# A two-layer hybrid decoder: the later projections with tokens stationary, and first loads and bias rows on other queues

## The chip, the cores and the metric

The kernel runs as one program on one core of a Trainium2 chip. The metric is the device time of the program in microseconds (us), as the median of several executions. One execution was also taken by the hardware profiler; all rows below come from it.

## The reference: what is computed

The input is x with 256 tokens of 2048 channels. Two layers follow each other, each with an RMS norm in front and a residual addition behind.

```python
h = rmsnorm(x, norm_g[0])                      # layer 0: dilated attention
proj = h @ a_w_in                              # 2048 x 20480
q, k, v of 3 groups x 16 heads x 128, z = split(proj)
q, k = head_rms(q) * gain, head_rms(k) * gain
o_g = softmax(q k^T / sqrt(128) + t5_bias, window and dilation of g) v
o = merge of the 3 groups by their softmax denominators
x = x + (o * silu(z)) @ a_w_out                # 2048 x 2048

h = rmsnorm(x, norm_g[1])                      # layer 1: Conformer convolution
a, ga, z = split(h @ b_w_in + b_in, 3)         # 2048 x 6144
u = causal_depthwise_conv(a * sigmoid(ga), width 31) + conv_b
u = layernorm(u) * ln_g + ln_b                 # over channels
x = x + (silu(u) * silu(z)) @ b_w_out + b_out  # 2048 x 2048
```

All of it is float32. The four weight matrices hold 30,720 rows of 2048 values, some 252 MB, and each is read once.

## The kernel before

**Chunks.** All weights come as 480 chunks of 128 x 1024 values (512 KB), read in a fixed order n: 320 for `a_w_in` (n below `N_A`), 32 for `a_w_out` (from `N_A` to `N_WO`), 96 for `b_w_in` (to `N_VI`), 32 for `b_w_out`. `stage(n)` (L108) fetches chunk n over SP's queue into `raw`, ScalarE (ACT) rounds it to `hi`, and `lo` = raw - hi is made by VectorE (DVE) or GpSimd (POOL), as `low_engine` (L92) says. Each of the three tiles has five buffers. The activations are split in the same way, and each product is three matmuls: high by high, low by high, high by low.

**The order is written by hand.** The main loop (L845 to L860) goes once over all chunks. For chunk n it stages chunk n + 3, issues the matmuls of chunk n, and then runs the functions that `at(n, ...)` has put at this step. Each engine works through its own instructions in this order, so an instruction that waits holds up all behind it on its engine. SP's queue holds the weight loads and all other loads and stores, with few exceptions.

**Attention stage (n below 320).** Eight sets of two heads, each with five column groups of eight chunks. `project` (L275) keeps 128 tokens stationary (`xh`, `xl`) and moves 512 weight columns, so a chunk is 12 matmuls of 512 columns into two accumulators of 128 tokens x 512. For q and k they are normalised, turned on TensorE by four transposes (`qk_turn`, L323) and split. The scores, softmax and values of the set before run between the chunks. The first eight chunks also load, scale and split x (`x_split`, L149; `load_first`, L154). From step 10 to 30 the T5 bias table is made in four parts: `bias_load` (L222) fetches a part of the one-hot and mask rows, `bias_rows` (L241) multiplies and adds, and `bias_store` (L250) writes it to memory over SP's queue. `load_bias` (L262) reads it back per head.

**The later stages.** `project_out` (L515) and `project_b` (L621) keep 128 x 128 weights stationary and move 256 tokens, so a chunk is 24 matmuls of 256 columns (L526 to L529 for the first half of an output projection, `products`, L537, elsewhere). Results have channels on the partitions. Accumulators come from four PSUM banks in turn (`acc`); two banks (`t`) take transposes and small sums, and `s` and `o` the scores and values.

- After `a_w_out`: `residual`, `square_sum`, `h_split` (L567 to L582) make x1, its squares' sum and the two parts of the second layer's input. The factor r1 of the norm is summed over partitions and spread to all of them by TensorE (`r1_sums`, `r1_spread`, L603 to L613), and is multiplied into every result of `b_w_in` (L646, L653, L797).
- Under `b_w_in` the convolution runs on VectorE: for each of 16 channel tiles 29 taps of 128 x 256 (`conv_tap`, L687), in two half sums in PSUM that are merged (L691). A list `line` with planned costs spreads them over the chunks (`run_line`, L636). POOL adds up the sums and squares for the layer norm (`gather`, L729). The mean of the first six tiles is taken off early (`mid_sums`). After the last tile `ln_sums` and, one chunk later, `ln_spread` (L744, L758) make the statistics with TensorE, VectorE and POOL, and `norm` and what follows it (L771 to L794) prepare the input of `b_w_out`, two channel tiles at a time.
- `store` (L826) adds x1 to each result and writes it over SP's queue, channels first; the host turns the output.

Of the kernel before, what the change touches and what calls it, by code (L numbers as in the profile page):

```python
# [17 lines left out]
P = 128  # L18
# [23 lines left out]
def hybrid_kernel(ctx: ExitStack, tc: tile.TileContext, x_perm, x_tok, x_nat, vecs, rel, onehot, maskrow,  # L42
                  w_in, w_out, v_in, v_out, out):
# [10 lines left out]

    def acc_tile(name):
        return bank("acc", name, 4)

    def t_tile(name):
        return bank("t", name, 2)
# [15 lines left out]
    units, z_next = [], 0  # L75
    for j in range(KT):
        units += [2 * j, 2 * j + 1]
        if j % 2 and j > 2:
            units.append(32 + z_next)
            z_next += 1  # L80
    units += [32 + j for j in range(z_next, KT)]

    def source(n):
        if n < N_A:
            return w_in[n]
        if n < N_WO:
            return w_out[n - N_A]
        if n < N_VI:
            return v_in[2 * units[(n - N_WO) // 2] + (n - N_WO) % 2]
        return v_out[n - N_VI]  # L90

    def low_engine(n):  # L92
        if n < N_WO + 8:
            return nc.gpsimd if N_A + 3 <= n < N_A + 16 else nc.vector
# [13 lines left out]
    def stage(n):  # L108
# [40 lines left out]
    def x_split(k, xr):  # L149
        g0 = vec[:, V_G0 + k:V_G0 + k + 1]  # L150
        nc.scalar.activation(xh[:, k, :], xr, AF.Copy, scale=g0)
        nc.vector.scalar_tensor_tensor(xl[:, k, :], xr, g0, xh[:, k, :].bitcast(F32), op0=ALU.mult, op1=ALU.subtract)  # L152

    def load_first():  # L154

        xr = apool.tile([P, 2, S], F32, tag="sc", name="xr0", bufs=2)
        raw, hi, lo = new_chunk(0)
        for i in range(2):
# [6 lines left out]
        for i in range(2):  # L165
            sl = slice(i * 512, (i + 1) * 512)
            nc.scalar.copy(hi[:, sl], raw[:, sl])
            x_split(i, xr[:, i, :])
            nc.vector.tensor_tensor(lo[:, sl], raw[:, sl], hi[:, sl].bitcast(F32), op=ALU.subtract)
# [52 lines left out]
    def bias_load(f):  # L222
        if f == 0:
            brow["rb"] = apool.tile([N_BUCKETS, NG * NH], F32, name="rb")
            nc.sync.dma_start(brow["rb"], rel)
            brow["oh"] = apool.tile([N_BUCKETS, 1024], F32, tag="bt", name="oh", bufs=2)
            brow["row"] = apool.tile([NH, 1024], F32, tag="bt", name="row", bufs=2)
            brow["oh_r"] = apool.tile([N_BUCKETS, 1024], F32R, tag="pp", name="oh_r", bufs=1)
        nc.sync.dma_start(brow["oh"], onehot[:, f * 1024:(f + 1) * 1024])
# [715 lines left out]
```

## Time and profile before

| | |
|---|---|
| median of 3 executions | 1452.47 us (1452.23 to 1452.49) |
| the profiled execution | 1452.36 us |
| its span in the trace | 1450.6 us |
| TensorE busy | 1442.3 us (99%) |
| VectorE, ScalarE, POOL busy | 960.2, 727.0, 423.7 us |
| DMA | 271.28 MB, mean 187 GB/s |

The span is the time from the first to the last instruction of the trace. Busy time is the time in which at least one instruction of the engine was at work. Matmuls overlap one another, so the durations of single matmuls add up to more than the time that they take.

### The profile page before, as it was taken

How to read it: one execution, taken by the hardware profiler on the slowest of the kernel's cores; microseconds unless marked ns; L12 is line 12 of the kernel's file. 1: busy time of each engine (PE TensorE's matmuls, PEld its weight loads, DVE VectorE, ACT ScalarE, POOL GpSimd, SP SyncE). 2: the span in 40 equal slices, each digit the busy share in tenths (PEclk: the TensorE clock that was granted, in tenths of full speed). 3: DMA queues.
4: the chain of work that ended last, by engine and by line, in shares of the span. 5: the costliest groups of instructions: out<-in, count | busy, mean ns of one | idle time of the engine just before them, and what ended most of it. 6: DMA issues, size and time to landing. Idle time of an engine off the chain costs nothing.

```text
span 1450.6 us, 22407 instructions
## 1 busy us (share of the span) xinstructions
PE 1442.3 (99%) x8524; PEld 1275.6 (88%) x8524; DVE 960.2 (66%) x1542; ACT 727.0 (50%) x1027; POOL 423.7 (29%) x339
## 2 busy tenths in 40 slices
PE   9999999999999999999999999999999999999999
PEld 7778888888888888888888888889999999999999
DVE  6656765765676576576567657646758989997621
ACT  7445554454455455445445545444545545555632
POOL 0210020011011002001001100207217979998544
PEclk9999999999999999999999999999999999999999
DMA  9458556557556655755755665566564655555544
GB/s 360 139 202 251 161 185 206 173 164 217 170 164 197 194 165 181 207 170 170 216 169 164 197 193 165 180 189 218 163 197 165 204 162 182 192 180 184 184 158 142
DMA packets 108699, 271.28 MB, mean 187 GB/s; under 512 B 42416, under 2 KB 44720, under 8 KB 108592
## 3 DMA queue, kind: packets, MB, share of 16 engines
q1 hardware_dynamic: 108160, 269.58, 58.2%
q8 instruction: 67, 1.10, 0.3%
q14 instruction: 40, 0.33, 0.1%
q10 hardware_dynamic: 432, 0.28, 0.1%
HBM read 267.46 MB, written 2.36 MB: 186 GB/s over the span
## 4 chain that ended last, share of the span: by engine, by line
PE 98%; DMA 1%; DVE 0%; ACT 0%; issue 0%; SPq 0%; POOL 0%; POOLq 0%; ACTq 0%
PE acc L290 60%; PE b L541 6%; PE b L542 6%; PE b L543 6%; PE psq L327 1%; PE wow L526 1%; PE vo L543 1%; PE vo L542 1%; PE vo L541 1%; PE vow L529 1%; PE vow L528 1%; PE vow L526 1%; PE wo L543 1%; PE wo L541 1%; PE wo L542 1%; PE wow L528 1%
## 5 line engine op out<-in xcount | busy, mean ns | idle before, releaser
L114 ACT CAST hi<-raw 128x1024 fp32r<-128x1024 f32 x479 | 497.0, 1048 | 292.7 <-PE acc L290 164.2
L117 DVE TENSOR_TENSOR lo<-raw,hi 128x1024 fp32r<-128x1024 f32 x358 | 441.3, 1234 | 282.2 <-ACT hi L114 275.7
L290 PE MATMUL acc<-hi,xh 128*128 128x512 f32 x1280 | 506.0, 397 | 0.1
L290 PE MATMUL acc<-lo,xh 128*128 128x512 f32 x1280 | 497.4, 391 | 0.8 <-DVE lo L117 0.8
L290 PE MATMUL acc<-hi,xl 128*128 128x512 f32 x1280 | 495.9, 389 | 0.0
L117 POOL TENSOR_TENSOR lo<-raw,hi 128x1024 fp32r<-128x1024 f32 x121 | 294.0, 2453 | 120.4 <-ACT hi L114 101.6
L290 PEld LDWEIGHTS acc<-lo,xh 128*128 128x128 f32 x1280 | 240.1, 188 | 53.4 <-DVE lo L117 1.2
L290 PEld LDWEIGHTS acc<-hi,xh 128*128 128x128 f32 x1280 | 240.5, 188 | 49.0 <-issue 2.0
L290 PEld LDWEIGHTS acc<-hi,xl 128*128 128x128 f32 x1280 | 240.8, 188 | 47.1 <-DVE xl L152 0.2
L129 POOL TENSOR_SCALAR rq<-ss 128x4 f32<-128x4 f32 x48 | 10.9, 226 | 789.7 <-DVE ss L309 787.8
L541 PE MATMUL b<-hh,hi 128*128 128x256 f32 x768 | 217.8, 284 | 0.0
L542 PE MATMUL b<-hl,hi 128*128 128x256 f32 x768 | 217.3, 283 | 0.0
L543 PE MATMUL b<-hh,lo 128*128 128x256 f32 x768 | 217.3, 283 | 0.0
L688 DVE SCALAR_TENSOR_TENSOR c<-u,vec,c 128x256 f32<-128x256 f32 x464 | 187.4, 481 | 3.5 <-ACT c L684 3.5
L542 PEld LDWEIGHTS b<-hl,hi 128*128 128x128 f32 x768 | 147.4, 192 | 0.0
L541 PEld LDWEIGHTS b<-hh,hi 128*128 128x128 f32 x768 | 147.4, 192 | 0.0
L543 PEld LDWEIGHTS b<-hh,lo 128*128 128x128 f32 x768 | 147.4, 192 | 0.0
L403 ACT ACTIVATE pr<-sc,m 128x512 f32<-128x512 f32 x32 | 23.1, 723 | 100.8 <-DVE m L401 100.8
L340 DVE TENSOR_TENSOR qk<-psq,qk 128x256 fp32r<-128x256 f32 x48 | 20.3, 422 | 50.6 <-ACT qk L339 50.6
L338 ACT CAST qk<-psq 128x256 fp32r<-128x256 f32 x48 | 17.9, 372 | 64.1 <-PE psq L327 63.6
L130 POOL TENSOR_TENSOR rq<-rq,nhalf 128x4 f32<-128x4 f32 x48 | 48.4, 1008 | 4.0
L422 ACT CAST pp<-pt 128x512 fp32r<-128x512 f32 x32 | 18.8, 587 | 44.1 <-PE pt L414 42.8
(167 smaller groups left out, 1668.0 us busy)
## 6 DMA issues: line engine op xcount, KB each, us to landing
raw<-w_in SPq DMA_DIRECT2D x319, 512.0 KB, 4.2
raw<-v_in SPq DMA_DIRECT2D x96, 512.0 KB, 3.3
raw<-w_out SPq DMA_DIRECT2D x32, 512.0 KB, 4.2
raw<-v_out SPq DMA_DIRECT2D x32, 512.0 KB, 4.1
bt<-btab SPq DMA_DIRECT2D x64, 128.0 KB, 5.8
x_tok<-x_tok SPq DMA_DIRECT2D x4, 512.0 KB, 9.4
x<-x_nat SPq DMA_DIRECT2D x4, 512.0 KB, 6.3
out_t<-ob SPq DMA_DIRECT2D x16, 128.0 KB, 1.8
```

Source lines behind the costliest of these rows:

```text
L114: nc.scalar.copy(hi, raw)
L117: low_engine(n).tensor_tensor(lo, raw, hi.bitcast(F32), op=ALU.subtract)
L130: nc.gpsimd.tensor_tensor(dst, dst, nhalf[:, :n], op=ALU.pow)
L290: nc.tensor.matmul(acc[b], lhsT=(xl if p == 1 else xh)[:, k, sl], rhs=wl if p == 2 else wh, start=k == 0 and p == 0, stop=k == KT - 1 and ...
L340: nc.vector.tensor_tensor(ql, ps[:, 0:2], qh.bitcast(F32), op=ALU.subtract)
L403: nc.scalar.activation(u.pr.rearrange("p a b -> p (a b)"), sc, AF.Exp, bias=u.m[:, 1:2], accum_out=u.m[:, 2:3])
L526: nc.tensor.matmul(acc, lhsT=wh, rhs=mh[:, m, :], start=m == 0 and ct % 2 == 0, stop=False, skip_group_check=True)
L528: nc.tensor.matmul(acc, lhsT=wh, rhs=ml[:, m, :], start=False, stop=False, skip_group_check=True)
L541: nc.tensor.matmul(acc, lhsT=wh, rhs=mh[:, k, :], start=k == 0, stop=False)
L542: nc.tensor.matmul(acc, lhsT=wh, rhs=ml[:, k, :], start=False, stop=False)
L543: nc.tensor.matmul(acc, lhsT=wl, rhs=mh[:, k, :], start=False, stop=k == KT - 1)
L688: nc.vector.scalar_tensor_tensor(c[t % 2], u[:, t:t + S], vec[:, cw + t:cw + t + 1], c[t % 2], op0=ALU.mult, op1=ALU.add)
```

## The change

All four parts of the change come together.

1. The three later projections keep 128 tokens stationary and move 512 weight columns, as the attention stage does: `three` and `pair` replace `products`. Weights are laid out for it by the host (`_groups`). Results now have tokens on the partitions.
2. So x1 is turned by TensorE for the second layer's input (`x_turn`), and each group of 512 columns of `b_w_in` is emptied by ACT with the factor r1 (`take_group`) and turned (`turn_group`). r1 is summed along the free axis by ACT (`accum_out`). The output needs no turn by the host, and the bias `b_out` is added as a row (`bias_fetch`, `bias_add`).
3. During `b_w_in` one of the four accumulator banks holds the sums of the layer norm, and VectorE adds them up there instead of POOL. The two half sums of a channel tile share one bank. `CHUNK`, the planner's time of a chunk, goes from 2.64 to 2.72.
4. The first three chunks are rounded and split in halves (`split_halves`); the first part of `vec` comes over POOL's queue; the one-hot and mask rows come in two whole loads, at steps 11 and 12, and the table's parts are stored over ACT's queue.

```diff
+    turns = {"acc": 0, "t": 0}
+    ring = [0, 1, 2, 3]
     def acc_tile(name):
-        return bank("acc", name, 4)
+        turns["acc"] += 1
+        return bank(f"acc{ring[turns['acc'] % len(ring)]}", name, 1)
...
     def stage(n):
...
         nc.sync.dma_start(raw, source(n))
+        if n < LEAD:
+            split_halves(n, raw, hi, lo, xr)
+            return
...
+    def split_halves(n, raw, hi, lo, xr):
+        for i in range(2):
+            sl = slice(i * 512, (i + 1) * 512)
+            nc.scalar.copy(hi[:, sl], raw[:, sl])
+            x_split(2 * n + i, xr[:, i, :])
+            nc.vector.tensor_tensor(lo[:, sl], raw[:, sl], hi[:, sl].bitcast(F32), op=ALU.subtract)
...
     def x_split(k, xr):
-        nc.scalar.activation(xh[:, k, :], xr, AF.Copy, scale=g0)
+        if k == 0:
+            nc.vector.tensor_scalar(xh[:, k, :], xr, g0, None, op0=ALU.mult)
+        else:
+            nc.scalar.activation(xh[:, k, :], xr, AF.Copy, scale=g0)
...
     def load_first():
+        nc.gpsimd.dma_start(vec[:, :V_HEAD], vecs[:, :V_HEAD])
...
-            if i == 0:
-                nc.scalar.dma_start(vec[:, :V_HEAD], vecs[:, :V_HEAD])
...
+            brow["oh"] = bpool.tile([N_BUCKETS, 4096], F32, tag="yl", name="oh")
+            nc.sync.dma_start(brow["oh"], onehot)
+        else:
+            brow["row"] = bpool.tile([NH, 4096], F32, tag="yh", name="row")
+            nc.sync.dma_start(brow["row"], bass.AP(tensor=maskrow.tensor, offset=maskrow.offset, ap=[[0, NH], [1, 4096]]))
...
     def bias_store(f):
-        nc.sync.dma_start(btab[:, f * 1024:(f + 1) * 1024], brow["row"])
+        sl = slice(f * 1024, (f + 1) * 1024)
+        nc.scalar.dma_start(btab[:, sl], brow["row"][:, sl])
-    for f in range(4):
-        at(10 + 5 * f, bias_load, f)
...
+    for i in range(2):
+        at(11 + i, bias_load, i)
+    for f, e in enumerate((17, 21, 23, 25)):
+        at(e - 1, bias_split, f)
+        at(e, bias_rows, f, 0)
+        at(e + 1, bias_rows, f, 1)
+        at(e + 2, bias_store, f)
...
+    def three(acc, xh_, xl_, wh, wl, first, last):
+        nc.tensor.matmul(acc, lhsT=xh_, rhs=wh, start=first, stop=False)
+        nc.tensor.matmul(acc, lhsT=xl_, rhs=wh, start=False, stop=False)
+        nc.tensor.matmul(acc, lhsT=xh_, rhs=wl, start=False, stop=last)
+    def pair(accs, hi, lo, kc, mh, ml, blocks_first):
+        order = [(i, b) for i in range(2) for b in range(2)]
+        if blocks_first:
+            order.sort(key=lambda x: x[1])
+        for i, b in order:
+            k, cs, ts = 2 * kc + i, slice(i * 512, (i + 1) * 512), slice(b * P, (b + 1) * P)
+            three(accs[b], mh[:, k, ts], ml[:, k, ts], hi[:, cs], lo[:, cs], k == 0, k == KT - 1)
...
+    def x_turn(q):
+        f.pt[q] = t_tile(f"px{q}").rearrange("p (c t) -> p c t", c=2)
+        for c in range(2):
+            for b in range(2):
+                ct = 2 * q + c
+                nc.tensor.transpose(f.pt[q][:, c, b * P:(b + 1) * P], f.x1[:, b, ct * P:(ct + 1) * P], ident)
...
     def project_b(n):
...
+        g, kc = divmod(n - N_WO, 8)
+        if kc == 0:
+            if g == 0:
+                ring[:] = [i for i in ring if i != 3]
+                open_convolution()
+            acc_b[g] = [acc_tile(f"b{g}_{b}") for b in range(2)]
+        pair(acc_b[g], hi, lo, kc, f.hh, f.hl, kc in (0, 7))
...
+    def take_group(g):
+        accs = acc_b.pop(g)
+        ev_b[g] = []
+        for b in range(2):
+            ev = f.pool.tile([P, 512], F32, tag="ev", name=f"ev{g}_{b}", bufs=4)
+            nc.scalar.activation(ev, accs[b], AF.Copy, scale=f.r1[:, b:b + 1])
+            ev_b[g].append(ev)
+    def turn_group(g, part, t):
+        ps = ps_g[g, part] = t_tile(f"pg{g}_{part}", t).rearrange("p (c t) -> p c t", c=2)
+        for c in range(2):
+            for b in range(2):
+                ct = 2 * part + c
+                nc.tensor.transpose(ps[:, c, b * P:(b + 1) * P], ev_b[g][b][:, ct * P:(ct + 1) * P], ident)
...
     def conv_first(j, u, cw, c):
-        tags = (("s", "o"), ("t", "t"))[j % 2]
-        c += [bank(tags[i], f"c{j}_{i}", 2 if tags[i] == "t" else 1)[:, :S] for i in range(2)]
+        ps = bank(("s", "o")[j % 2], f"c{j}", 1)
+        c += [ps[:, :S], ps[:, S:]]
...
+    def gather(j, sq):
+        out_ = f.sb if j == KT - 1 else f.sums
+        if j > HALF_J:
+            nc.vector.tensor_tensor(out_[:, S:], f.sums[:, S:], f.d[:, j, :], op=ALU.add)
+        nc.vector.tensor_tensor(out_[:, :S], f.sums[:, :S], sq, op=ALU.add)
+        if j == KT - 1:
+            ring[:] = [0, 1, 2, 3]
+            at(f.n + 1, ln_sums)
...
+    for g in range(NB):
+        e = N_WO + 8 * g + 7
+        at(e, take_group, g)
+        if g < NGLU:
+            at(e + 1, turn_group, g, 1, 1)
+            at(e + 1, turn_group, g, 0, 0)
+            at(e + 2, glu, g)
         else:
...
+            for part in range(2):
+                at(e + 1 + 2 * part, turn_group, g, part, 1)
+                at(e + 2 + 2 * part, z_silu, g, part)
+    def store(cg):
+        accs = oacc.pop(cg)
+        for b in range(2):
+            o = f.pool.tile([P, 512], F32, tag="ev", name=f"ob{cg}_{b}", bufs=4)
+            for h in range(1 + (cg == 3 and b == 1)):
+                sl = slice(h * S, (h + 1) * S) if cg == 3 and b == 1 else slice(0, 512)
+                c0 = cg * 512
+                nc.vector.tensor_tensor(o[:, sl], accs[b][:, sl], f.x1[:, b, c0 + sl.start:c0 + sl.stop], op=ALU.add)
+                (nc.sync, nc.scalar)[h].dma_start(out[b * P:(b + 1) * P, c0 + sl.start:c0 + sl.stop], o[:, sl])
```

## Rows read from the trace of the kernel before

**Rows 1.** The page: busy time of the engines, and the chain by engine.

```profile
PE 1442.3 (99%) x8524; PEld 1275.6 (88%) x8524; DVE 960.2 (66%) x1542; ACT 727.0 (50%) x1027; POOL 423.7 (29%) x339
...
PE 98%; DMA 1%; DVE 0%; ACT 0%; issue 0%; SPq 0%; POOL 0%; POOLq 0%; ACTq 0%
```

**Rows 2.** Waits of TensorE: for whom, us in total, times, longest.

```profile
PE psq L327 <- DVE qn L319: 1.4, 1, 1.4
...
PE psq L327 <- DVE row L248: 0.8, 1, 0.8
```

**Rows 3.** Groups by form: out<-in, xcount | busy us, mean ns | idle before.

```profile
L327 PE MATMUL psq<-ident,qn 128*128 128x128 f32 x192 | 28.9, 273 | 2.2 <-DVE qn L319 1.4 <-DVE row L248 0.8
```

**Rows 4.** The chain in the attention stage: start us, us, what.

```profile
215.63 0.44 PE psq L327 x4
216.07 2.78 PE acc L290 x12
...
219.29 38.13 PE acc L290 x168
```

**Rows 5.** Timeline of TensorE, and the last addition: start us, us, what.

```profile
215.47 0.60 PE L327 MATMUL psq<-ident,qn 128*128 128x128 f32 x4
215.82 0.48 PE L290 MATMUL acc<-hi,xh 128*128 128x512 f32 x1
...
1355.19 0.28 PE L526 MATMUL vow<-bh,hi 128*128 128x256 f32 x1
...
1447.23 0.28 PE L543 MATMUL vo<-bh,lo 128*128 128x256 f32 x1
...
1447.55 0.42 DVE L828 TENSOR_TENSOR ob<-vo,x 128x256 f32<-128x256 f32 x1 [5.33 <-PE vo L543]
```

**Rows 6.** SP's wait for the table (us, times, longest), and ACT behind it.

```profile
SPq L251 <- DVE row L248: 48.6, 4, 13.5
...
89.31 1.05 ACT L114 CAST hi<-raw 128x1024 fp32r<-128x1024 f32 x1 [7.25 <-DMA raw<-w_in]
```

**Rows 7.** Timeline of the start, and small loads: KB, us to landing.

```profile
5.25 0.51 ACT L151 ACTIVATE xh<-xr,vec 128x256 fp32r<-128x256 f32 x1 [0.34 <-DMA vec<-vecs]
5.66 0.60 ACT L167 CAST hi<-raw 128x512 fp32r<-128x512 f32 x1
6.19 0.68 DVE L169 TENSOR_TENSOR lo<-raw,hi 128x512 fp32r<-128x512 f32 x1
...
7.87 1.05 ACT L114 CAST hi<-raw 128x1024 fp32r<-128x1024 f32 x1 [1.11 <-DMA raw<-w_in]
9.36 0.88 DVE L152 SCALAR_TENSOR_TENSOR xl<-xr,vec,xh 128x256 fp32r<-128x256 f32 x2 [1.48 <-ACT xh L151]
11.43 0.73 PE L290 MATMUL acc<-lo,xh 128*128 128x512 f32 x2 [0.80 <-DVE lo L117]
...
vec<-vecs ACTq DMA_DIRECT2D x1, 19.0 KB, 4.0
rb<-rel SPq DMA_DIRECT2D x1, 6.0 KB, 10.1
```

**Rows 8.** Timeline of the layer norm's statistics: VectorE and TensorE.

```profile
1334.98 2.34 DVE L755 SCALAR_TENSOR_TENSOR rn<-st_ln,rn 128x2 f32<-128x2 f32 x1 [1.12 <-POOL rn L130]
1336.09 0.60 PE L600 MATMUL ps_rn<-ident,rn 128*128 128x128 f32 x4
1337.37 0.71 PE L600 MATMUL ps_rn<-ident,rn 128*128 128x128 f32 x4 [0.68 <-DVE rn L755]
```

**Rows 9.** Taps by group and in order of time; a window's busy us by engine.

```profile
L688 DVE SCALAR_TENSOR_TENSOR c<-u,vec,c 128x256 f32<-128x256 f32 x464 | 187.4, 481 | 3.5 <-ACT c L684 3.5
...
1201.33 2.04 DVE L688 SCALAR_TENSOR_TENSOR c<-u,vec,c 128x256 f32<-128x256 f32 x5
...
1110.00:1320.00 210.00, 210.00 (x1753) 210.00 (x1753) 192.91 (x487) 111.92 (x164) 195.68 (x116) 1.00 0.56 184
```

**Rows 10.** ACT's copy of a whole bank out of PSUM, as a group.

```profile
L349 ACT ACTIVATE vh<-acc,r 128x512 fp32r<-128x512 f32 x16 | 10.8, 688 | 8.5 <-PE acc L290 8.5
```

More of the change, by code (lines that the diff above doesn't have):

```diff
@@ L71, in at @@
         steps.setdefault(n, []).append((fn, args))
[L75 to L81, printed above, removed]
+    NGLU = 8
+    NB = 12
     def source(n):
@@ L161, in load_first @@
             nc.scalar.dma_start(xr[:, i:i + 1], x_perm[:, i:i + 1, :])
-            if i == 0:
-                nc.scalar.dma_start(vec[:, :V_HEAD], vecs[:, :V_HEAD])
         warm_up()
[L165 to L169, printed above, removed]
+        split_halves(0, raw, hi, lo, xr)
     def load_x(c):
@@ L238, in bias_split @@
             nc.vector.tensor_tensor(brow["lo"], brow["rb"], brow["hi"].bitcast(F32), op=ALU.subtract)
-        nc.scalar.copy(brow["oh_r"], brow["oh"])
+        brow["oh_r"] = apool.tile([N_BUCKETS, 1024], F32R, tag="pp", name=f"oh_r{f}", bufs=1)
+        nc.scalar.copy(brow["oh_r"], brow["oh"][:, f * 1024:(f + 1) * 1024])
     def bias_rows(f, half):
@@ L537, in products @@
-    def products(acc, hi, lo, half, mh, ml):
-        for i in range(8):
-            k = half * 8 + i
-            wh, wl = hi[:, i * P:(i + 1) * P], lo[:, i * P:(i + 1) * P]
-            nc.tensor.matmul(acc, lhsT=wh, rhs=mh[:, k, :], start=k == 0, stop=False)
-            nc.tensor.matmul(acc, lhsT=wh, rhs=ml[:, k, :], start=False, stop=False)
-            nc.tensor.matmul(acc, lhsT=wl, rhs=mh[:, k, :], start=False, stop=k == KT - 1)
+                for cg in range(2):
+                    oacc[cg] = [acc_tile(f"{tag}{cg}_{b}") for b in range(2)]
@@ new lines, in open_convolution @@
+    def open_convolution():
+        f.sums = bank("acc3", "sums", 1)
+        f.u = []
+        for i in range(2):
+            u = bpool.tile([P, 8, TAPS - 1 + S], F32, tag=("yh", "yl")[i], name=f"u{i}")
+            nc.gpsimd.memset(u[:, :, :TAPS - 1], 0.0)
+            f.u += [u[:, j, :] for j in range(8)]
+    def take_group(g):
+        accs = acc_b.pop(g)
+        ev_b[g] = []
+        for b in range(2):
+            ev = f.pool.tile([P, 512], F32, tag="ev", name=f"ev{g}_{b}", bufs=4)
+            nc.scalar.activation(ev, accs[b], AF.Copy, scale=f.r1[:, b:b + 1])
+            ev_b[g].append(ev)
@@ L637, in run_line @@
         clock[0] = max(clock[0], now)
-        while line and clock[0] < now + 2.64:
+        while line and clock[0] < now + CHUNK:
             cost, fn, args = line.pop(0)[1:]
@@ L823, in hybrid_kernel, with z_silu @@
-    for j in range(KT):
-        at(N_WO + 12 + 3 * j, add_bias, j)
-    def store(ct):
-        o = f.pool.tile([P, S], F32, tag="ob", name=f"ob{ct}", bufs=8)
-        nc.vector.tensor_tensor(o, oacc.pop(ct), f.x1[:, ct, :], op=ALU.add)
-        if ct == KT - 1:
-            nc.sync.dma_start(out[ct], o)
-        else:
-            at(f.n + 1, nc.sync.dma_start, out[ct], o)
-    for ct in range(KT):
-        if ct < 8:
-            at(N_VI + KT - 1, store, ct)
-        else:
-            at(N_VI + KT + 2 * (ct - 8) + 1, store, ct)
+    def z_silu(g, part):
+        ps = ps_g.pop((g, part))
+        for c in range(2):
+            j = 4 * (g - NGLU) + 2 * part + c
+            nc.scalar.activation(f.gate[:, j, :], ps[:, c], AF.Silu, bias=vec[:, V_BIN + 32 + j:V_BIN + 33 + j])
@@ L841, in hybrid_kernel @@
+    for cg, m in enumerate((15, 15, 23, 31)):
+        at(N_VI + m, store, cg)
     make_identity(nc, ident)
```

279 lines of the change are left out of this document (115 added, 164 removed).

## The prediction

> **What bounds the kernel now.** I read the page first. TensorE is busy 99% of the span, and it is 98% of the chain that ended last [rows 1]. So the time is the sum of what TensorE issues, plus its few waits. Next I read whom TensorE waited for. Behind the start-up the waits are 1.4, 0.8 and 0.7 us [rows 2, 8]. Nothing off TensorE counts unless it makes TensorE wait.
>
> Then I looked for what one product costs. Its own duration is no price: 0.28 us for 256 columns, though the 768 products of the last projection start between 1355.19 and 1447.23, which is 0.1200 us each [rows 5]. The time from start to start is what is paid. A chunk of 24 such products takes 2.88 us. In the attention stage 168 products of 512 columns take 38.13 us behind a transpose, and 38.13/14 less the 0.06 found below is 2.72 us for a chunk of 12, or 0.2267 us each [rows 4]. Twice 0.1200 less 0.2267 is 0.0133: each product pays this fixed part beside its columns, and 512 columns pay it once.
>
> **The change, part by part.**
>
> *Wide products.* All 160 chunks behind the first projection (32, 96, 32) go from 24 products of 256 to 12 of 512 on the same data: 160 x (2.88 - 2.72) = -25.6 us. The form is the one that the attention stage already runs. The Trainium skill, TensorE: Matmul & The Clock Gate, section Back-to-back issue gap, gives columns/2.4 GHz + 2.5 ns, so 109 and 216 ns; by that, as an estimate, a chunk would save 0.03 us, the stages 5.0 us, and the whole change would lose. The trace has 120 and 227 ns, so I go by the rows.
>
> *Transposes come in.* The result now has tokens on the partitions, so 32 of x1 (x_turn, 8 bouts of four), 64 for the GLU groups (8 bouts of eight) and 32 for the gate groups (8 bouts of four) are added: 128, all on TensorE. The nearest row is the attention stage's turn of q and k: a bout of four (0.44) and the chunk behind it (2.78) take 3.22 against 2.72, so 0.50 a bout [rows 4]. A second four directly behind adds no change of kind; four of them cost 0.35 between starts (215.47 to 215.82 [rows 5]), so 0.86 for eight. 16 x 0.50 + 8 x 0.86 = +14.9 us. Bounds: 0.35 a four if no change of kind were paid, 11.2 in all; 128 times the mean duration of 0.273, 34.9 us [rows 3], if nothing overlapped. I take 14.9, for the same instruction stood in the same kind of stream. The Trainium skill, same page, section Part 4: PE-mode transpose, counts about 275 ns for one in a kernel; the row has 273 as the duration but four in 0.44.
>
> *The norm's sums.* r1 now comes from accumulators on ACT with tokens on partitions, so two bouts go, the token sums and the spread; each is taken as a bout of four, 0.44 [rows 4]. -0.9 us.
>
> *Bias table.* SP stood 48.6 us in front of four stores of the table, once 13.5 us, with the weight loads queued behind [rows 6]. Then ACT sat idle 7.25 us for a weight chunk, VectorE's queue ran late, and TensorE waited 1.4 for qn and 0.8 for the row [rows 2, 6]. The profile ends a product some 0.16 us after its slot (0.28 against 0.12 [rows 5]), so the two cost 2.2 + 0.3 = 2.5 us. Now the mask and one-hot rows come whole, ahead, and the store stands on ACT. There the next hi copies wait behind it, but for the addition of one step before, and they are needed four chunks later (11 us). The row load waits on SP for the square of the last token tile, with raw16 behind it; that chunk is used some 15 us later. -2.5 us; bounds -2.5 and 0.
>
> *First chunks.* Chunk 1's weights land at 7.87; hi, xh, xl and lo follow whole, and TensorE's stream is unbroken only from 11.43 with the seventeenth product [rows 7]. So it runs as if it had begun at 11.43 - 16 x 0.2267 = 7.80. In halves: hi 0.60, xh 0.51, xl 0.45 and the lower half 0.68 [rows 7] put that product's operand at 10.12; the second half's comes 1.1 later, before product 23 wants it at 11.5. That is a start of 6.5: -1.25 us. Chunk 2 needs its last half at 14.3 and by the same durations has it at 13.5. vec now comes over POOL's queue; over ACT's it took 4.0 us, and the slowest small load took 10.1 [rows 7]. From its landing to chunk 1's first lower half VectorE does 3.9 us of work, so the start is the landing + 0.3, and a landing before 6.2 costs nothing. Issued near 1.4, it lands near 5.4 at 4.0 us, and at 11.5 at worst: start 11.8, +4.0 instead of -1.25. I take -1.25.
>
> *VectorE under the second projection* hides all the convolution work. It is busy 192.9 of 210 us there now, POOL 195.7 [rows 9]. It loses 48 scalings of 256 (r1 is applied by ACT as it empties the bank). It gains the running sums that POOL did, 29 additions of 0.42 (the size of the last line of [rows 5]), and 4 more lower parts ahead of the convolution. Its sum: 464 taps x 0.39 (five took 2.04, the last of them 0.48 [rows 9]) = 182, the sums 12, some 48 more of 0.42 (GLU, merges, one wide subtraction) 20: 214 us. The convolution starts later, near 27 us into the stage, since its first group takes 8 chunks, then a turn. Each later group waits for its turn, the last till 185.6 us (65 chunks x 2.72, 8 x 0.86 of turns, 0.9 for the first half's mean, 1.0 for the sigmoid and GLU). Behind it 143 taps and 9 us of rest are left by the written order: 185.6 + 65 = 251. TensorE asks for the statistics after chunk 89, at 90 x 2.72 + 6.9 + 5 x 0.50 + 0.9 = 255. So VectorE is 4 us early and the cost 0. Both half sums now share one PSUM bank; no row shows taps in turn on one bank, so a tap lies between 0.39 and its whole duration, 0.48. I take 0.39, for each tap already reads and writes one bank at once.
>
> *The norm of the convolution* keeps its wait. VectorE's tiny rn took 2.34 us, and the second spread started 0.92 us after the first had gone (1336.09 + 0.36 to 1337.37) [rows 8]. Between the sums and the spread lie now 2.78 and a gate bout of 0.50 instead of 2.9: -0.3 us; bounds -0.9 and +3 (VectorE late).
>
> *A new wait.* With the ring of three banks, group 11 ends in banks 0 and 1, and the ring of four then hands bank 1 first to the last projection. TensorE must wait till ACT has emptied it: 0.20 us until the result can be read (1447.23 + 0.12 to 1447.55 [rows 5]), 0.69 for the copy of 512 [rows 10], a hand-over: +1.0 us. Behind it stands all of TensorE; if a hi copy stands before it, +2.0; if the evacuation is hidden, 0. Elsewhere the half-chunk order (block 0 first) gives 1.36 us, more than such a copy.
>
> *The end.* The last block is added in two halves of 0.42 [rows 5], the second stored by ACT: +0.4 us; bounds 0 and 0.9.
>
> *Sum:* -25.6 + 14.9 - 0.9 - 2.5 - 1.25 - 0.3 + 1.0 + 0.4 = -14.25. The profiled execution took 1452.36 us, 1.76 of it outside the span, and the median is 1452.47. So 1452.4 - 14.2 = **1438.2 us**. All lower bounds together give 1432. The upper ones without the rivals' (eights at 1.00, no gain from the bias, half of the late vec, the last three terms at +3, +2 and +0.9) give 1449.
>
> **Rivals.**
> *VectorE becomes the bound (the other side).* If a tap on one bank costs 0.48, 321 taps ahead of the last group (27 + 149 + 28 us, with 23 of rest among the 149) and 143 behind it (78) end at 282 instead of 251. TensorE waits 27 us at the statistics: 1465. From 0.45 us a tap on the change is slower than before. For it: VectorE is 92% busy there now. Against it: it loses 48 operations, and nothing in a tap changes but the address. 0.06.
> *The gap scales with the columns.* If 512 columns cost 0.240 here, the 25.6 is gone: 1463.8. The page's gap rule named above would leave 5.0 of it: 1458.8. Against both: 1280 x 3 products of this form run at 0.227. 0.02.
> *Turns are waited for.* If ACT or VectorE is late with the operands, each of 24 bouts can cost a copy of 0.69 [rows 10]: up to +16.6, 1454.8. For it: ACT stands in order behind copies that wait for taps. Against it: a whole chunk (2.72) lies between evacuation and turn. Part of it (1441 to 1449) 0.13, all of it 0.02.
> *Vec is late* over POOL's queue: +5.25, 1443.5. 0.07.
>
> **How the numbers follow.** The forecast has 0.70, with 1435 to 1441 as its own range. Late vec and partly waited turns (0.20) are still faster than before. The slower cases hold 0.06 + 0.02 + 0.02 = 0.10. About 0.2% (2.9 us) is what a measurement of this kernel can tell from no change, and the cases hardly stop there: faster 0.88, same 0.02, slower 0.10. The range is 1435 to 1445: it takes in late vec and half of the partly waited turns.
>
> **What would show it.** Products of 512 columns in all stages 0.227 us apart; 3.22 us from the start of a gate bout to the end of the chunk behind it; the unbroken stream as if begun at 6.5 us; no wait for qn or row near 90 us; the waits that are left at the identity, the spread and bank 1, each near 1 us; taps 0.39 apart, and VectorE idle before the statistics. It is wrong if taps lie 0.45 apart, if TensorE shows waits at px or pg, or if VectorE stands busy while TensorE waits for the sums.

## The result, and the profile after

The changed kernel takes 1496.08 us (median of 4, 1494.71 to 1498.35), the kernel before 1452.48 us beside it: ratio 1.0301, 95% interval 1.0289 to 1.0314. It is 3% slower; 1438.2 us was forecast, and 1435 to 1445 as the range. The profiled execution took 1496.78 us, its span is 1495.0 us.

The page after, to be set against [rows 1]: busy time by engine, the clock granted to TensorE in 40 slices (tenths of 2.4 GHz), and the chain that ended last.

```profile
PE 1453.4 (97%) x6724; PEld 1198.2 (80%) x6724; DVE 1006.2 (67%) x1514; ACT 733.7 (49%) x1038; POOL 379.2 (25%) x279
...
PEclk9999999999999999999999999999999989998999
...
PE 79%; DVE 9%; issue 5%; POOL 4%; ACT 2%; DMA 1%; POOLq 0%; DVEq 0%; SPq 0%; ACTq 0%
```

The share of TensorE in the chain fell from 98 to 79%, VectorE's rose from 0 to 9, and the clock has lower slices in the last quarter. The stages say where the time went. A stage runs from its first product to the next one's; the forecast's terms are put on the stages that they fall in. The last column is an experiment told below.

| stage, us of span | before | forecast | changed | taps in pairs |
|---|---|---|---|---|
| attention, to the first product of `a_w_out` | 973.6 | 969.9 | 969.6 | 970.3 |
| `a_w_out` | 100.7 | 98.6 | 99.8 | 99.8 |
| `b_w_in` | 280.9 | 276.2 | 331.1 | 280.7 |
| `b_w_out` and the end | 95.4 | 91.7 | 94.5 | 94.3 |
| span | 1450.6 | 1436.4 | 1495.0 | 1445.1 |

The attention stage came out as forecast. Of the 58.6 us between forecast and result 54.9 lie in one stage, the second projection with the convolution under it.

There the taps answer to [rows 9]. First their group, then VectorE's order of time, then the same window of 210 us (after its length: PE, PEld, DVE, ACT, POOL busy, clock, DMA share, GB/s):

```profile
L735 DVE SCALAR_TENSOR_TENSOR c<-u,vec,c 128x256 f32<-128x256 f32 x464 | 227.0, 489 | 16.4 <-ACT c L732 1.5
```

```profile
1131.30 0.42 DVE L744 TENSOR_TENSOR d<-c,half 128x256 f32<-128x256 f32 x1 [0.44 <-ACT half L741]
1132.10 15.18 DVE L735 SCALAR_TENSOR_TENSOR c<-u,vec,c 128x256 f32<-128x256 f32 x29
1147.71 0.43 DVE L744 TENSOR_TENSOR d<-c,half 128x256 f32<-128x256 f32 x1 [0.44 <-ACT half L741]
```

```profile
1110.00:1320.00 210.00, 186.95 (x784) 150.17 (x783) 189.96 (x402) 95.16 (x140) 138.60 (x60) 0.93 0.50 148
```

Twenty-nine taps take 15.18 us: (15.18 - 0.49) / 28 = 0.525 us from tap to tap, where five took 2.04 before, 0.39 from tap to tap. The mean duration hardly moved (481 to 489 ns). What went is the overlap of neighbouring taps, and a gap of 0.035 us came (the 16.4 us of idle time over 464 taps). From its first tap at 1099.1 to its last at 1375.4 VectorE stops for little but that gap and the copies of the half sums (0.44 us each).

TensorE's waits behind the first product of this stage (us, times, longest), its products after one of them (start us, us), and the 3.3 us behind that wait (columns as in the window above):

```profile
PE b L530 <- ACT ev L674: 9.1, 3, 5.6
PE b L532 <- POOL lo L122: 9.0, 6, 1.7
PE sums L212 <- ACT sb L751: 4.7, 1, 4.7
PE b L530 <- ACT hi L119: 4.4, 4, 2.5
PE ps_ln L212 <- DVE sb L791: 3.4, 1, 3.4
```

```profile
1151.12 0.50 PE L532 MATMUL b<-lo,hh 128*128 128x512 f32 x1 [1.71 <-POOL lo L122]
...
1153.38 0.63 PE L532 MATMUL b<-lo,hh 128*128 128x512 f32 x1
1153.80 0.63 PE L530 MATMUL b<-hi,hh 128*128 128x512 f32 x1
1154.23 0.63 PE L531 MATMUL b<-hi,hl 128*128 128x512 f32 x1
...
1155.34 0.39 PE L531 MATMUL b<-hi,hl 128*128 128x512 f32 x1
1155.57 0.39 PE L532 MATMUL b<-lo,hh 128*128 128x512 f32 x1
```

```profile
1151.70:1155.00 3.30, 3.30 (x9) 2.61 (x8) 3.12 (x8) 2.89 (x4) 3.30 (x2) 0.50 0.62 173
```

The whole stage in the same columns:

```profile
1069.40:1400.50 331.10, 298.14 (x1273) 240.77 (x1271) 285.94 (x570) 153.02 (x225) 201.98 (x91) 0.94 0.50 150
```

Only 3.4 us of waiting shows where a late VectorE would be looked for, at the sums of the norm. The rest is spread: TensorE waits for staged weights and for banks to be emptied. Behind the wait shown here, the second within 3 us, the products start 0.425 us apart for 3.3 us, with the granted clock at 0.50 (1.2 GHz), before they come back to 0.23. Added up, the waits of this stage are some 33 us (4 with the taps in pairs, told below), and a granted clock of 0.94 over 331.1 us is some 20 us more: 49 of the 50 us by which the stage is longer than it is there. ACT's waits tell why the weights were late (us, times, longest):

```profile
ACT lsq L779 <- DVE d L744: 64.9, 9, 11.8
ACT half L741 <- DVE c L735: 52.8, 7, 10.3
```

ACT stands in its written order at copies and squares that need the slow taps, and the rounding of the next chunks stands behind them.

### The profile page after: what moved, and what is told of

It is laid out like the page before. It is cut to its first block, busy times and chain, and to the rows that moved or that the text cites. A ratio compares the mean times of both kernels' runs of the same rounds, so it can differ in the third digit from the quotient of the medians.

```text
span 1495.0 us, 18609 instructions
## 1 busy us (share of the span) xinstructions
PE 1453.4 (97%) x6724; PEld 1198.2 (80%) x6724; DVE 1006.2 (67%) x1514; ACT 733.7 (49%) x1038; POOL 379.2 (25%) x279
## 4 chain that ended last, share of the span: by engine, by line
PE 79%; DVE 9%; issue 5%; POOL 4%; ACT 2%; DMA 1%; POOLq 0%; DVEq 0%; SPq 0%; ACTq 0%
PE acc L303 59%; DVE c L735 7%; POOL lo L122 4%; PE b L532 2%; PE b L530 2%; PE b L531 2%; PE wo L530 2%; PE wo L532 2%; PE wo L531 2%; PE psq L340 1%; PE vo L532 1%; PE vo L530 1%; PE vo L531 1%; PE pt L427 1%; ACT hi L119 1%
## 5 line engine op out<-in xcount | busy, mean ns | idle before, releaser
L735 DVE SCALAR_TENSOR_TENSOR c<-u,vec,c 128x256 f32<-128x256 f32 x464 | 227.0, 489 | 16.4 <-ACT c L732 1.5
L530 PE MATMUL b<-hi,hh 128*128 128x512 f32 x384 | 158.4, 412 | 13.5 <-ACT ev L674 9.1
L532 PE MATMUL b<-lo,hh 128*128 128x512 f32 x384 | 156.8, 408 | 9.0 <-POOL lo L122 9.0
L531 PE MATMUL b<-hi,hl 128*128 128x512 f32 x384 | 155.5, 405 | 0.0
L530 PEld LDWEIGHTS b<-hi,hh 128*128 128x128 f32 x384 | 76.1, 198 | 31.7 <-ACT ev L674 10.7
L532 PEld LDWEIGHTS b<-lo,hh 128*128 128x128 f32 x384 | 75.8, 198 | 28.4 <-POOL lo L122 11.9
L531 PEld LDWEIGHTS b<-hi,hl 128*128 128x128 f32 x384 | 75.8, 197 | 15.5
L353 DVE TENSOR_TENSOR qk<-psq,qk 128x256 fp32r<-128x256 f32 x48 | 20.3, 422 | 51.1 <-ACT qk L352 51.0
L530 PE MATMUL vo<-hi,bh 128*128 128x512 f32 x128 | 50.1, 392 | 1.6 <-ACT ev L674 1.6
L530 PE MATMUL wo<-hi,yh 128*128 128x512 f32 x128 | 51.4, 401 | 0.0
L532 PE MATMUL vo<-lo,bh 128*128 128x512 f32 x128 | 50.3, 393 | 1.0 <-POOL lo L122 0.9
```

The lines of the kernel that those rows point to most:

```text
L353: nc.vector.tensor_tensor(ql, ps[:, 0:2], qh.bitcast(F32), op=ALU.subtract)
L530: nc.tensor.matmul(acc, lhsT=xh_, rhs=wh, start=first, stop=False)
L531: nc.tensor.matmul(acc, lhsT=xl_, rhs=wh, start=False, stop=False)
L532: nc.tensor.matmul(acc, lhsT=xh_, rhs=wl, start=False, stop=last)
L735: nc.vector.scalar_tensor_tensor(c[t % 2], u[:, t:t + S], vec[:, cw + t:cw + t + 1], c[t % 2], op0=ALU.mult, op1=ALU.add)
```

## The experiments

Theory A: the two half sums share one bank, so each tap waits for the tap just before it instead of the last but one. A tap costs 0.13 us more, 464 x 0.13 = 61 us, and VectorE is the bound. Rival B: the stage of wide products loses the time itself (banks emptied by ACT, turns, clock), beside slow taps. Rival C: it is the shared bank that is slow, not the wait. Rival D: ACT's standing in order is the loss.

In the program's own list of waits, nearly every tap of the changed kernel waits for the count of the instruction directly in front of it on VectorE, and in the kernel before for the count of the last but one. The tile framework sets these waits: for two halves of one bank it makes one chain, for two halves of a tile in SBUF, as the next run shows, two.

**The taps by themselves**

```diff
+    ways = [
+        (b0[:, :S], b1[:, :S]),
+        (b2[:, :S], b3[:, :S]),
+        (b4[:, :S], b4[:, S:]),
+        (b5[:, :S], b5[:, :S]),
+        (b6[:, :S], mixed1),
+        (two0, two1),
+        (sb_one[:, :S], sb_one[:, S:]),
+    ]
...
+    def run(c):
+        for t in range(2, TAPS):
+            src = c[(t + (c is ways[1])) % 2]
+            nc.vector.scalar_tensor_tensor(c[t % 2], u[:, t:t + S], w[:, t:t + 1], src, op0=ALU.mult, op1=ALU.add)
```

> Not the whole computation: only chains of 29 taps of 128x256 on VectorE, one chain after the other, with the two half sums placed in seven ways, first with GpSimd idle, then again beside GpSimd's 128x1024 subtractions. Theory A (a tap that must wait for the tap just before it cannot overlap it): two PSUM banks in turn (two_a, two_b) 0.39 us from tap to tap as before the change; the two halves of one bank (one) 0.52 us as after it; one sum alone (single) 0.52 us; two banks where each tap reads what the one before wrote (ping, pong) also 0.52 us, because the wait and not the bank costs. Rival C (the bank is slow when neighbouring taps use it, not the wait): ping, pong 0.39 us, one and single 0.52 us. For the half sum in SBUF no row stands: theory A expects 0.36 to 0.42 us where two tiles take turns (mixed, sb_two), and the same for two halves of one SBUF tile (sb_one), since there each tap waits only for the tap before last. Beside GpSimd the PSUM chains stay within 0.03 us of this if the two engines do not disturb each other.

VectorE's order of time, GpSimd idle:

```profile
7.15 0.48 DVE L54 SCALAR_TENSOR_TENSOR two_b<-u,w,two_b 128x256 f32<-128x256 f32 x1
7.55 0.48 DVE L54 SCALAR_TENSOR_TENSOR two_a<-u,w,two_a 128x256 f32<-128x256 f32 x1
...
18.64 0.49 DVE L54 SCALAR_TENSOR_TENSOR pong<-u,w,ping 128x256 f32<-128x256 f32 x1
19.17 0.49 DVE L54 SCALAR_TENSOR_TENSOR ping<-u,w,pong 128x256 f32<-128x256 f32 x1
...
33.21 15.18 DVE L54 SCALAR_TENSOR_TENSOR one<-u,w,one 128x256 f32<-128x256 f32 x29
48.30 15.18 DVE L54 SCALAR_TENSOR_TENSOR single<-u,w,single 128x256 f32<-128x256 f32 x29
63.40 0.48 DVE L54 SCALAR_TENSOR_TENSOR mixed<-u,w,mixed 128x256 f32<-128x256 f32 x1
63.79 0.48 DVE L54 SCALAR_TENSOR_TENSOR mixed_sb<-u,w,mixed_sb 128x256 f32<-128x256 f32 x1
...
86.29 11.56 DVE L54 SCALAR_TENSOR_TENSOR sb_one<-u,w,sb_one 128x256 f32<-128x256 f32 x29
```

Two banks in turn: 0.39 us from tap to tap. The halves of one bank: 15.18 us for 29, to the digit the row of the changed kernel. One sum alone: the same. Two banks where each tap reads what the one before wrote: 0.525, so the wait alone makes the price and no shared bank is needed; rival C is out as the cause. Two halves of one tile in SBUF: (11.56 - 0.48) / 28 = 0.396, since there the program waits for the last but one. Taps on one PSUM bank without the wait were not tried, so what the bank by itself would cost stays open.

Beside GpSimd the PSUM chains keep these times. The one with a sum in SBUF does not:

```profile
98.16 92.07 POOL L67 TENSOR_TENSOR lo<-raw,hi 128x1024 fp32r<-128x1024 f32 x40
...
154.46 0.48 DVE L54 SCALAR_TENSOR_TENSOR mixed<-u,w,mixed 128x256 f32<-128x256 f32 x1
154.85 35.65 DVE L54 SCALAR_TENSOR_TENSOR mixed_sb<-u,w,mixed_sb 128x256 f32<-128x256 f32 x1
190.43 0.48 DVE L54 SCALAR_TENSOR_TENSOR mixed<-u,w,mixed 128x256 f32<-128x256 f32 x1
```

Its first tap whose two tensor operands lie in SBUF stood 35.65 us, until GpSimd's last subtraction was over at 190.2, some 15 of them on.

**The odd half sum in SBUF**

```diff
-        c += [ps[:, :S], ps[:, S:]]
+        c += [ps[:, :S], f.pool.tile([P, S], F32, tag="c1", name=f"c1_{j}", bufs=2)]
```

> The changed kernel with one edit: the odd taps' half sum is a tile in SBUF, the even taps' half sum keeps its half bank. Theory A (the shared bank makes each tap wait for the one before, VectorE becomes the bound, and all else of the loss follows): taps 0.39 to 0.42 us apart, VectorE's taps shorter by 464 x 0.11 to 0.13 = 51 to 60 us, second projection's stage back from 331 us to about 276 to 280 us, time 1438 to 1444 us, ratio to before 0.990 to 0.994. If a tap into SBUF is dearer (0.45 us) VectorE stays the bound and the time is 1455 to 1470 us. Rival B (the loss comes from the wide products' stage itself: ScalarE emptying banks, transposes, TensorE's clock, with the slow taps only beside it): at most 10 us come back, 1485 to 1496 us.

1571.54 us (1570.47 to 1572.16), ratio 1.0818 (1.0802 to 1.0835): far from both expectations. The taps' group (before the bar: us in all, mean ns):

```profile
L735 DVE SCALAR_TENSOR_TENSOR c<-u,vec,c 128x256 f32<-128x256 f32 x464 | 322.8, 770 | 1.0 <-ACT c L731 1.0
```

The mean went from 489 to 770 ns although no tap waits for the one before. In this stage GpSimd makes the lower parts, and the taps stand beside them as in the run above: 79 of the 464 took 1.1 to 2.5 us, each beside one of GpSimd's subtractions and ending some 0.28 us behind it; no other took more than 0.49. Eight taps beside four subtractions:

```profile
1144.16 10.32 DVE L735 SCALAR_TENSOR_TENSOR c<-u,vec,c 128x256 f32<-128x256 f32 x8
1144.26 9.93 POOL L122 TENSOR_TENSOR lo<-raw,hi 128x1024 fp32r<-128x1024 f32 x4 [4.84 <-ACT hi L119]
```

Here, unlike in the run above, one tap gets in behind each subtraction although the next one follows at once. I had not seen the stand coming, and as a test between A and B the run says nothing; that slower taps cost more time it does show.

**The kernel before, with the halves of one bank**

```diff
-        tags = (("s", "o"), ("t", "t"))[j % 2]
-        c += [bank(tags[i], f"c{j}_{i}", 2 if tags[i] == "t" else 1)[:, :S] for i in range(2)]
+        ps = bank(("s", "o")[j % 2], f"c{j}", 1)
+        c += [ps[:, :S], ps[:, S:]]
```

> The kernel before with one edit, the part of the change that theory A blames: both half sums of a channel tile in the two halves of one bank. Theory A: taps 0.52 us apart, 464 x 0.13 = 60 us more on VectorE, which had some 4 us to spare, so 1452.5 + 50 to 57 = 1502 to 1510 us. Rival B (the placement is hidden and the new projection loses the time): 1452 to 1456 us.

1488.86 us (1488.70 to 1489.73), ratio 1.0252 (1.0234 to 1.0269): +36 us from this part alone, without one wide product or turn. Rival B is out as the whole cause.

```profile
L688 DVE SCALAR_TENSOR_TENSOR c<-u,vec,c 128x256 f32<-128x256 f32 x464 | 226.7, 488 | 18.8 <-ACT c L685 4.8
```

The size was expected at 50 to 57. First to last tap went from 236.3 us (1091.1 to 1327.4) to 273.2, so 36.9 and not 61. By their group the taps took 54.6 us more (226.7 + 18.8 against 187.4 + 3.5 in [rows 9]), and 18 of these were taken up inside the stretch, where VectorE had stood idle 20.3 of the 236.3 us, mostly waiting for TensorE's results, which in that kernel it takes out of PSUM itself. I had counted only the 4 us at the end as room. In the changed kernel the first tap comes 29.7 us into the stage instead of 16.9, and there was hardly any such room.

**The half sums copied by VectorE**

```diff
-            nc.scalar.copy(half, c[1])
+            nc.vector.tensor_copy(half, c[1])
```

> The changed kernel with one edit: the seven copies of the odd half sum (for channel tiles 0 to 6) run on VectorE, so that ScalarE does not stand in its order waiting for taps there. Theory A: VectorE's own sum of work sets the end of the stage, so the time stays within 1488 to 1497 us (7 x 0.44 us of waiting for ScalarE leave VectorE), though TensorE's waits move from the staged weights towards the sums of the norm. Rival D (ScalarE standing in order starves the weight staging and drops TensorE's clock, and that is the loss): 1475 us or less.

1496.99 us (1496.23 to 1497.56), ratio 1.0306 (1.0290 to 1.0321): the same as the changed kernel. TensorE's waits only changed places:

```profile
PE b L530 <- ACT ev L674: 14.8, 4, 5.6
PE sums L212 <- ACT sb L751: 6.4, 1, 6.4
PE b L532 <- POOL lo L122: 4.3, 3, 1.7
```

So the spread waits and the clock that falls behind them are how the delay reaches TensorE, not its source. Rival D is out for the copies. ScalarE's waits at the squares stayed (65.0 us), so for them this run decides nothing; against them stands that VectorE's taps follow one another almost without a stop, their last one ending 306 us into the stage in both kernels, and the next run, which alters the order of the taps and leaves ScalarE its copies and squares.

**Taps of two channel tiles in turn**

```diff
-        for t in range(2, TAPS):
-            line.append((("tap", j), 0.4, conv_tap, (u, cw, c, t)))
-        line.append((("merge", j), 0.7, conv_merge, (j, c)))
+        held.append((j, u, cw, c))
+        if j % 2:
+            for t in range(2, TAPS):
+                for jj, uu, ww, cc in held:
+                    line.append((("tap", jj), 0.4, conv_tap, (uu, ww, cc, t)))
+            for jj, uu, ww, cc in held:
+                line.append((("merge", jj), 0.7, conv_merge, (jj, cc)))
+            held.clear()
```

(The squares get eight buffers instead of two, and the first taps of tile 8 stand ahead of the seven squares.)

> The changed kernel with only the order of the taps altered: the 29 taps of two channel tiles take turns, so that neighbouring taps lie in different banks and each waits for the tap before last, though both half sums of a tile still share a bank (seven squares get seven more buffers for it). Theory A (the wait for the tap just before is the whole loss): taps 0.39 us apart, VectorE from first to last tap about 212 to 222 us instead of 276 (464 x 0.13 = 60 us less, up to 8 us more where the next pair's first two taps by ScalarE are waited for), so it ends about 10 us earlier against the stage than in the kernel before and TensorE sets the time again: 1438 to 1443 us, second projection's stage 276 to 279 us. Rival B (the wide products' stage loses the time itself): 1485 us or more. Rival E (the first tap comes 12.8 us later in the stage than before the change, and this alone makes VectorE the bound): 1446 to 1460 us with taps at 0.39 us.

1447.16 us (1446.43 to 1448.82), ratio 0.9966 (0.9953 to 0.9978), and in a second run beside other kernels, the tenth experiment:

> The paired taps once more, the same kernel as before, to have its time beside the one above on the same chip: 1446.4 to 1448.8 us as measured. It also tells whether the 3 us between the kernels that evacuate first (1450 us) and the paired taps (1447 us) belong to the edit or to the run: if the edit, this one stays near 1447 us.

1447.22 us (1445.89 to 1447.70), ratio 0.9962 (0.9949 to 0.9974). Of the 58 us between result and forecast 49 are back, though the half sums of a tile still share a bank. Neighbouring taps now lie in different banks, so it is the chains above and not this run that tell the wait from the bank. The taps' group, the start of VectorE's taps, and the window:

```profile
L742 DVE SCALAR_TENSOR_TENSOR c<-u,vec,c 128x256 f32<-128x256 f32 x464 | 184.4, 485 | 6.6 <-ACT c L739 6.6
```

```profile
1100.67 5.58 DVE L742 SCALAR_TENSOR_TENSOR c<-u,vec,c 128x256 f32<-128x256 f32 x14 [0.46 <-ACT c L739]
```

```profile
1110.00:1320.00 210.00, 208.65 (x957) 172.10 (x956) 192.92 (x489) 115.80 (x167) 171.29 (x73) 1.00 0.60 181
```

Fourteen taps in 5.58 us are 0.39 each, the clock is 1.00 again, and the stage takes 280.7 us. By the two groups the wait costs 52 us in this kernel (227.0 + 16.4 against 184.4 + 6.6), not 61: in the written order a paired tap takes 0.41 on the mean and not 0.39. First to last tap is 225.7 us instead of 276.4 (212 to 222 expected). VectorE ends its taps at 1325.4, 255.4 us into the stage, and the last sum for the norm at 258.6; TensorE asks for the sums at 258.8. It no longer waits there, with 0.2 us to spare. So rival E of that expectation (the late first tap alone) is out too: it used up the room and cost nothing.

TensorE's waits behind the first product of the stage that are left, where 1438 to 1443 us had been expected:

```profile
PE vo L530 <- ACT ev L674: 1.9, 1, 1.9
PE b L530 <- ACT ev L674: 1.3, 2, 1.0
PE ps_rn L624 <- DVE rn L817: 1.0, 1, 1.0
PE vo L532 <- POOL lo L122: 0.8, 2, 0.5
```

**What is left between 1447 and the forecast**

Six runs took such waits, or terms of the sum, one by one. The constants back on ScalarE's queue:

```diff
-        nc.gpsimd.dma_start(vec[:, :V_HEAD], vecs[:, :V_HEAD])
...
+            if i == 0:
+                nc.scalar.dma_start(vec[:, :V_HEAD], vecs[:, :V_HEAD])
```

> The kernel with paired taps and one more edit: the first vector constants go back from GpSimd's queue to ScalarE's, between the two halves of the first tokens, as before the change. Theory (their landing at 6.60 us sets the first product): they land at about 4.0 us, the first product comes at 6.2 to 6.5 us instead of 7.1, and the time falls by 0.6 to 0.9 us against the paired taps alone. Rival (the second half of the first tokens, then behind the constants on the same queue, comes later and takes it back): within 0.3 us of the paired taps alone.

1446.97 us (1445.50 to 1448.97), ratio 0.9962 (0.9947 to 0.9977): no difference. The constants were there at 5.21 us instead of 6.15, and the first product came 0.94 us earlier (5.71 against 6.65). Of that 0.48 us were left at the ninth chunk, because the first three products then started 0.43 to 0.57 us apart. The medians do not show it: in the second run of the pairs, the same kernel, the constants were there only at 6.92 and the first product came at 7.42.

ScalarE empties a group's banks ahead of the next split (on top of that):

```diff
...
+        if n in early:
+            project_b(n)
+            take_group((n - N_WO) // 8)
         if n + LEAD < N_ALL:
             stage(n + LEAD)
...
```

> The paired taps with the constants on ScalarE's queue, and one more edit: behind the last chunk of each group of the second projection ScalarE empties the two banks before it splits the next staged chunk, not after. Theory (one 128x1024 split of 1.0 us stands ahead of the evacuation, and with three banks in the ring TensorE waits for it: 1.2 us in two gate groups and 1.9 us ahead of the last projection's first product): these waits fall by about 1 us each, 1.5 to 3 us in all, against 1447.0 us. Rival (the splits that are now 1.25 us later, or GpSimd's lower parts behind them, make TensorE wait elsewhere): no gain, within 0.5 us.

1450.34 us (1449.09 to 1452.97), ratio 0.9986 (0.9976 to 0.9995): 3 us worse than the pairs. In the profile the bank waits fell from 3.1 to 1.5 us, and new ones came:

```profile
1216.67 0.50 PE L531 MATMUL b<-hi,hh 128*128 128x512 f32 x1 [0.53 <-ACT hi L119]
...
1219.10 0.50 PE L533 MATMUL b<-lo,hh 128*128 128x512 f32 x1 [1.69 <-POOL lo L122]
```

The norm's statistics read from PSUM (on top of that, then on the pairs alone):

```diff
-        nc.vector.scalar_tensor_tensor(f.rn[:, 2:4], st[:, :2], -1.0, f.rn[:, :2], op0=ALU.mult, op1=ALU.mult)
+        nc.vector.scalar_tensor_tensor(f.rn[:, 2:4], f.ps[:, :2], -1.0 / D, f.rn[:, :2], op0=ALU.mult, op1=ALU.mult)
```

> The same and one more edit: the three tiny operations behind the norm's sums read the sums from PSUM, so that none has two operands in SBUF. Theory (VectorE cannot run an operation with two SBUF operands beside GpSimd's subtraction; the 128x2 product took 2.30 us and ended as GpSimd's chunk did): that operation takes 0.2 us, TensorE's wait for the second spread (1.0 us) goes, and the time falls by 1.0 to 1.5 us. Rival (the 2.3 us are the operation's own): nothing changes.

> The paired taps with the three tiny operations of the norm's statistics reading the sums from PSUM, and nothing else. In the trace of the paired taps TensorE stood 1.4 us between the two spreads for a 128x2 product of 2.30 us. Theory: that wait goes, 0.5 to 1.5 us less than the paired taps on the same chip, 1445.5 to 1447 us. Rival (GpSimd's chunk, which the power operation of the same chain stands behind, takes the place of the wait): within 0.4 us.

1449.72 us (1448.50 to 1451.30), ratio 0.9980 (0.9971 to 0.9989), and 1447.43 us (1446.47 to 1448.34), ratio 0.9963 (0.9949 to 0.9977): nothing that can be measured either time. The operation itself did what was expected, set against the first of [rows 8]; this is the first of the two kernels, with GpSimd's subtraction beside it and VectorE's next operation:

```profile
1334.67 2.37 POOL L122 TENSOR_TENSOR lo<-raw,hi 128x1024 fp32r<-128x1024 f32 x1
...
1334.73 0.16 DVE L818 SCALAR_TENSOR_TENSOR rn<-ps_ln,rn 128x2 f32<-128x2 f32 x1 [2.07 <-POOL rn L142]
1334.81 3.31 DVE L122 TENSOR_TENSOR lo<-raw,hi 128x1024 fp32r<-128x1024 f32 x1
```

The operation that had taken 2.30 us with the taps in pairs now takes 0.16, and TensorE's wait for the second spread went. The stand did not go but moved: the lower part behind it, the next operation with two operands in SBUF, takes 3.31 us, where it took 1.21 before. In the second kernel the bank wait ahead of the last projection's first product grew from 1.9 to 2.9 us in its place.

The evacuation first behind the gate groups only:

> The paired taps with the statistics read from PSUM, and ScalarE empties the banks before it splits the next staged chunk behind the four gate groups alone (where every group did so, TensorE gained 1.6 us of bank waits and lost 2.2 us to late splits and lower parts near 1216 us, among the GLU groups, and 1.2 us in the last projection). Theory: the bank waits of the gate groups (1.2 us) and of the last projection's first product (2.9 us) fall by 2 to 3 us together and nothing else changes: 1444.5 to 1446 us. Rival (each split that steps back is missed later, here too): within 1 us of 1447.3 us, with the waits for lower parts in the last projection grown.

1448.34 us (1447.10 to 1448.75), ratio 0.9967 (0.9955 to 0.9979): no gain. The gate groups' waits fell from 1.2 to 0.6 us, the one ahead of the last projection is still 2.4: there the split of a chunk was not in the way, but two activations of the norm that wait 1.1 us for VectorE.

And one part of the change undone, on the kernel that evacuates first: the bias table's stores on SP's queue again.

```diff
-        nc.scalar.dma_start(btab[:, sl], brow["row"][:, sl])
+        nc.sync.dma_start(btab[:, sl], brow["row"][:, sl])
```

> The kernel that evacuates first, with one part of the change undone: the four stores of the bias table stand on SP's queue again, among the weight loads, not on ScalarE's. Theory of the forecast (SP standing in front of these stores delays the weights, worth up to 2.5 us): waits for qn or the row come back near 90 us and the time rises by 1 to 2.5 us. Rival (loading the rows whole and earlier did it, the queue of the store does not matter): within 0.5 us.

1450.28 us (1449.78 to 1452.81), ratio 0.9986 (0.9977 to 0.9995): the same as without. SP again stands 36.3 us in front of them; the first of [rows 6] has 48.6:

```profile
SPq L264 <- DVE row L260: 36.3, 4, 12.3
```

TensorE's waits near 90 us do not come back, but for 0.2 us. Since rows and one-hot now come whole and ahead, the store's queue no longer matters.

## Why the prediction was wrong, step by step

- **VectorE under the second projection: the step that failed.** It said that a tap on the shared bank lies "between 0.39 and its whole duration, 0.48", and took 0.39, "for each tap already reads and writes one bank at once". It is 0.525, above both bounds. The argument looked at the memory; what counts is whom a tap waits for. The whole duration was no upper bound either, because a tap that waits starts 0.035 us after its predecessor's end. The rest of that step held only just: with the taps in pairs the first tap came 29.7 us into the stage (27 forecast), VectorE's last sum was ready at 258.6 (251 forecast) and TensorE asked at 258.8 (255 forecast), so of 4 us of room 0.2 were there.
- **The rival "VectorE becomes the bound" is what happened.** It had 0.06 and stopped at 0.48 and 1465 us. By its own sum a tap of 0.525 gives 27 + 23 + 9 + 464 x 0.525 = 303 us instead of 251, 48 us of waiting and 1486 us; measured, VectorE's last sum was ready at 308 and the kernel took 1496. The reason against it, "nothing in a tap changes but the address", was wrong: the order of waits changed with the address.
- **Wide products**: 0.227 us apart, as forecast, in all three stages. (The 5.0 us that this step names beside its own sum, and the 1458.8 of the second rival, come out as 4.8 and 1459.0; neither sum nor chances move by it.)
- **Transposes**: four cost 0.46 us beside products (0.50 forecast), eight 0.90 (0.86): 14.6 us against 14.9. From the start of a gate bout to the end of the chunk behind it are 3.18 to 3.21 us (3.22 forecast). Their operands were never late where the taps were paired.
- **Bias table**: both waits near 90 us are gone. The attention stage is 4.0 us shorter, 3.3 with the taps in pairs; less the gain of the first chunks below that leaves 3.4 and 2.3 where 2.5 was forecast. (In the other runs of the changed kernel and its variants this stage takes 968.7 to 971.5 us.) But the store's queue, half of the reason given, has no share in it.
- **First chunks**: the first product of the ninth chunk came 0.58 us earlier (29.12 against 29.70), 1.01 with the taps in pairs and 0.24 in that kernel's second run; 1.25 forecast. The constants were there at 6.60, 6.15 and 6.92 us, not near 5.4.
- **Bank 1 ahead of the last projection**: 1.6 to 2.9 us where ScalarE's order is as written (0.9 to 2.4 where it evacuates first), 1.0 forecast. Two more such waits, in gate groups, had not been seen: the 1.36 us of the other block's products are not enough when ACT splits a chunk first.
- **The norm's spread**: 1.59 us from one spread to the next with the taps in pairs, 1.28 before; -0.3 was forecast. **The end**: 4.4 us from the last product's start to the end of the span, 3.4 before, 0.4 more forecast.

The pairs miss the forecast by 9 us. The table puts 4.5 of them in the second projection (some 3 are bank waits, of which 1.0 was forecast, and 1.0 is the wait for the norm's spread), 2.6 behind it and 1.2 in `a_w_out`. What each wait would give back alone stays open: where a run removed one, another of like size came in its place, or a late split that cost more.

The forecast's other half, that the three projections are worth having, holds in a smaller size: with the taps in pairs the change is 5.3 us faster than the kernel before, and that version is faster than both.

## What to carry to other kernels

Two accumulators that are used in turn hide part of each other's time only while no instruction waits for the one just before it. When such tiles are moved together, look first at which instruction each one waits for in the program, and take the price from a chain that waits (0.525 us) and not from the duration (0.48) or the memory. And count an engine's room where it lies: idle time inside the stretch can be used, and a later first instruction takes it away.

## What the runs showed of the hardware

- **Consecutive instructions of VectorE overlap by about a fifth if they may.** 128x256 with a duration of 0.48 us start 0.39 us apart; a wait for the one before makes it 0.525, in one bank or in two. The Trainium skill, VectorE: DVE Perf Modes, section The DRAIN you can't avoid, reports eight copies that took as long with a semaphore after each as with one at the end; for these taps the runs differ, by 0.13 us each, and the measurement decides.
- **An operation with two tensor operands in SBUF stands while GpSimd subtracts.** Beside a stream of subtractions one tap stood 35.65 us and ended with it; in the kernel with a half sum in SBUF 79 taps stood for one subtraction each, up to 2.5 us; a 128x2 operation took 2.30 us beside one subtraction and 0.16 with one operand in PSUM. The Trainium skill, SBUF — State Buffer, section SBUF: two separate sides, calls the port pair of the two engines an exclusive lock that is held for an instruction. The runs agree that VectorE stands beside GpSimd's subtractions, and the 79 taps that one instruction is the measure. That a wait can go on over some 15 of them in a row is what the chains add; why it did so there and not in the kernel stays open. With one half sum in SBUF the kernel took 1571.5 us instead of 1496.1.
